# Two-layer hybrid decoder trunk: another order of the first loads, warm-up on a constant, constants in two transfers

## The chip, the cores and the metric

The kernel runs on one core of one Trainium2 chip. The metric is the device time of one execution in microseconds (us); a version's time is the median of its runs. Beside the times stands one profiled execution, whose records are quoted as rows. Engines: PE is TensorE (PEld its weight loads), ACT is ScalarE, DVE is VectorE, POOL is GpSimd, SP is SyncE; a "q" behind the name means the engine's instruction queue, which also issues transfers.

## The reference

`x` is 256 tokens by 1024 channels, float32, and there are two layers. Each layer does this, cut to what matters:

```python
hn = rms_norm(x, norm_gain)
proj = jnp.einsum('bsd,de->bse', hn, w_in)          # 1024 -> 3584 columns
a_q, a_k, a_v, a_g, b_x, b_g, c_q, c_k, c_v, c_g = jnp.split(proj, _in_split_points(), axis=-1)
y_a = dilated_attention(rope(a_q), rope(a_k), a_v) * silu(a_g)      # 8 heads of 64
y_b = rg_lru_branch(b_x, conv_w, ..., lru_lambda) * silu(b_g)       # 256 channels
y_c = stick_breaking_attention(c_q, c_k, c_v) * silu(c_g)           # 4 heads of 64
return x + jnp.einsum('bse,ed->bsd', concatenate([y_a, y_b, y_c], -1), w_out)
```

A last `rms_norm` follows the two layers. The value columns `a_v` (512 columns) and `c_v` (256 columns) are what the kernel projects first.

## The kernel before, in words

**Products.** Every float32 product of the projections is made of three fast-format products. An operand is split into a rounded part `hi` and a rest `lo`; ACT (or DVE) rounds, DVE subtracts, and PE adds hi*hi, lo*hi and hi*lo into one PSUM bank. So each weight tile that arrives costs ACT one pass, DVE one pass and PE three matmuls.

**The head of layer 0** (lines 129 to 173) is where the change lies. The 1024 channels are taken in eight steps `k` of 128. What step `k` needs comes as one packed row block `first[k]` of 128 x 1024: columns 0 to 255 are x transposed (S = 256), columns 256 to 767 the 512 value columns of `a_v`, and columns 768 to 1023 the 256 columns of `c_v`. It lands in a staging tile `st`, of which there are five in turn. Step 0 differs: its x comes with the eight columns of gains as a transfer of its own, `x0` (132 KB, line 133), and its weights as three pieces of 128 KB into `st0` (lines 134 to 136), issued in turn from ACT's and SP's queues. Steps 1 to 7 are single 512 KB transfers from SP's queue (line 147); a later one waits until the staging tile that it overwrites is free.

In a step, ACT writes `xh`, the rounded x times gain (line 155); `whi` is rounded by DVE for the 512 value columns in steps 0 and 1, in two pieces in step 0 (line 157), and by ACT for the rest (lines 159 and 161); DVE makes `xl` (line 162) and `wlo` (line 164). Step 0 is 18 matmuls of 256 columns, a later step 6 of 512 and 6 of 256 (line 171). In steps 0 and 1 PE goes through all columns for xh*hi, then for xl*hi, then for xh*lo; from step 2 on it finishes the 512 value columns first.

Before the first data is there, PE runs seven matmuls of 512 bf16 columns on a tile `cold` that DVE has set to zero (lines 129, 130 and 142). Their result is never read.

**After the head**, SP issues in this order: `prm_t`, the two halves of the first weight chunk CQ (line 107), the four pieces of `xres` (line 181), the constants `con` as one transfer of 128 x 640 (line 186), the rope table `rp` (line 399), the gate weights `gw_t` (line 401), and then the weight chunks CK and on, each in halves of 512 KB, as staging tiles come free (line 107). `con` holds a band `diag` and the identity `ident` in columns 0 to 255 and the mask `nmask` in columns 256 to 639. `ident` is first read when DVE spreads the inverse norms on a diagonal (line 380), `nmask` by the attention scores (line 525).

**Order.** PE's instructions run in the order in which the source writes them; those of the other engines are ordered by the framework's scheduler. The framework adds the waits, for data, for free buffers, and for the semaphores of its transfers.

Of the kernel before, what the change touches and what calls it, by code (L numbers as in the profile page):

```python
# [11 lines left out]
BF16 = mybir.dt.bfloat16  # L12
# [3 lines left out]
P = 128  # L16
S = 256
# [20 lines left out]
C_NM = 256  # L38
C_W = 640
# [10 lines left out]
def trunk_kernel(ctx: ExitStack, tc: tile.TileContext, x, first_x, first, wpack, prm_d, gatew, gains, consts, rope, out):  # L50
    nc = tc.nc
    act, dve, pe, gps = nc.scalar, nc.vector, nc.tensor, nc.gpsimd
# [4 lines left out]
    sb = ctx.enter_context(tc.tile_pool(name="sb", bufs=1))  # L57
# [19 lines left out]
    def table(name, behind=()):  # L77
        load = act.preload_act_table_set(name)  # L78
        for u in (*loaded["users"], *behind):
            dep(load, u)  # L80
        loaded["load"], loaded["users"] = load, []
# [44 lines left out]
        ask(l, c, ahead)  # L126
        return ready.pop((l, c))

    cold = sb.tile([P, 512], BF16, name="cold", tag="th")
    dve.memset(cold, 0.0)  # L130
    x0 = sb.tile([P, S + NK], F32, name="x0", tag="it")
    st0 = wst.tile([P, 1024], F32, name="st", tag="st")
    nc.sync.dma_start(out=x0, in_=first_x)
    act.dma_start(out=st0[:, S:S + 256], in_=first[0][:, S:S + 256])
    nc.sync.dma_start(out=st0[:, S + 256:S + 512], in_=first[0][:, S + 256:S + 512])
    act.dma_start(out=st0[:, S + 512:1024], in_=first[0][:, S + 512:1024])
    table(LN_EXP)
    av_ps = [bank(at, "s") for _ in range(NT)]
    cv_bk = [bank(pp, "pp") for _ in range(NT)]
# [42 lines left out]
    con = cst.tile([P, C_W], F32, name="con")  # L182
    ident = con[:, C_ID:C_ID + P]
    nmask = con[:, C_NM:C_NM + 384]
    diag = con[:, C_DG:C_DG + 255]
    nc.sync.dma_start(out=con, in_=consts)

    tiny_t = cst.tile([P, 48], F32, name="tiny")
    tiny = tiny_t[:, 0:1]
# [111 lines left out]
    for l in range(L):  # L301
# [254 lines left out]
        th = sb.tile([P, 2, S], F32, name="th", tag="th")  # L556
# [264 lines left out]
```

## Time and profile before

| what | value |
|---|---|
| median of 3 runs | 246.11 us (245.97 to 247.12) |
| profiled execution | 246.3 us, its recorded span 244.4 us |
| PE busy | 237.7 us, 97% of the span |
| DVE / ACT busy | 193.6 us (79%) / 170.7 us (70%) |
| first matmul on data | 4.73 us after the span's start |
| moved by transfers | 43.90 MB, mean 180 GB/s |

The profiled execution has 1.9 us outside its recorded span. Times in rows count from the span's start. A row of the timeline gives start, duration, engine, line, operation, destination and sources, and in square brackets how long the engine was idle before and what ended that. Rows that follow each other directly on one engine are merged, with their count.

### The profile page before, as it was taken

How to read it: one execution, taken by the hardware profiler on the slowest of the kernel's cores; microseconds unless marked ns; L12 is line 12 of the kernel's file. 1: busy time of each engine (PE TensorE's matmuls, PEld its weight loads, DVE VectorE, ACT ScalarE, POOL GpSimd, SP SyncE). 2: the span in 40 equal slices, each digit the busy share in tenths (PEclk: the TensorE clock that was granted, in tenths of full speed). 3: DMA queues.
4: the chain of work that ended last, by engine and by line, in shares of the span. 5: the costliest groups of instructions: out<-in, count | busy, mean ns of one | idle time of the engine just before them, and what ended most of it. 6: DMA issues, size and time to landing. Idle time of an engine off the chain costs nothing.

```text
span 244.4 us, 4800 instructions
## 1 busy us (share of the span) xinstructions
PE 237.7 (97%) x1777; PEld 213.0 (87%) x1777; DVE 193.6 (79%) x457; ACT 170.7 (70%) x371; POOL 10.9 (4%) x43
## 2 busy tenths in 40 slices
PE   7999999999999999999999999999999999999991
PEld 3889999999998899878889988888889889987881
DVE  3884699999999889986693665999999967885262
ACT  3759969628788499974672775876679749993143
POOL 0037000002000000000000000000010000000000
PEclk9999999999999999999999999999999999999999
DMA  7989989366836841277359387605471862000022
GB/s 209 400 259 388 398 279 331 119 206 182 265 119 207 310 112 71 90 237 257 107 161 258 108 305 255 200 6 192 155 215 27 241 253 86 3 0 0 3 75 97
DMA packets 14038, 43.90 MB, mean 180 GB/s; under 512 B 1728, under 2 KB 3008, under 8 KB 14016
## 3 DMA queue, kind: packets, MB, share of 16 engines
q1 hardware_dynamic: 13248, 42.43, 52.1%
q10 hardware_dynamic: 576, 0.66, 0.7%
q0 software_dynamic: 192, 0.52, 0.7%
q8 instruction: 14, 0.23, 0.4%
q14 instruction: 8, 0.07, 0.1%
HBM read 42.03 MB, written 1.05 MB: 176 GB/s over the span
## 4 chain that ended last, share of the span: by engine, by line
PE 96%; DMA 1%; ACT 1%; issue 0%; DVE 0%; DVEq 0%
PE pp L215 51%; PE pp L334 11%; PE s L215 9%; PE pp L331 5%; PE s L171 5%; PE s L465 3%; PE pp L171 2%; PE y L429 2%; PE s L518 2%; DMA x<-first_x 1%; PE s L445 1%; PE y L215 1%; PE pp L429 1%; PE s L577 1%; PE s L263 1%
## 5 line engine op out<-in xcount | busy, mean ns | idle before, releaser
L112 DVE TENSOR_TENSOR wlo<-st,whi 128x512 fp32r<-128x512 f32 x132 | 84.1, 686 | 13.9 <-ACT whi L110 13.6
L110 ACT ACTIVATE whi<-st 128x512 fp32r<-128x512 f32 x132 | 73.5, 627 | 17.1 <-PE pp L215 7.1
L215 PE MATMUL pp<-xx,whi 128*128 128x256 f32 x480 | 63.3, 285 | 0.0
L215 PEld LDWEIGHTS pp<-xx,whi 128*128 128x128 f32 x480 | 59.6, 191 | 0.8 <-issue 0.3
L215 PE MATMUL pp<-xx,wlo 128*128 128x256 f32 x240 | 33.7, 283 | 0.0
L215 PEld LDWEIGHTS pp<-xx,wlo 128*128 128x128 f32 x240 | 31.0, 192 | 0.0
L334 PE MATMUL pp<-xx,whi 128*128 128x512 f32 x112 | 29.3, 396 | 0.0
L334 PEld LDWEIGHTS pp<-xx,whi 128*128 128x128 f32 x112 | 20.1, 189 | 3.8 <-ACT scr L84 0.3
L84 ACT ACTIVATE pr<-scr,mn 128x128 f32<-128x128 f32 (+1 forms) x32 | 14.1, 442 | 6.6 <-DVE mn L525 6.6
L78 ACT ACT_TABLE_LOAD x13 | 16.7, 1283 | 1.9 <-PEq L814 1.7
L331 PEld LDWEIGHTS pp<-xx,wlo 128*128 128x128 f32 x112 | 15.3, 190 | 1.1
L331 PE MATMUL pp<-xx,wlo 128*128 128x256 f32 x112 | 15.6, 282 | 0.0
L215 PE MATMUL pp<-whi,yh 128*128 128x512 f32 (+1 forms) x48 | 13.3, 382 | 0.0
L215 PE MATMUL pp<-wlo,yh 128*128 128x512 f32 (+1 forms) x48 | 12.8, 372 | 0.0
L215 PE MATMUL pp<-whi,yl 128*128 128x512 f32 (+1 forms) x48 | 12.8, 372 | 0.0
L417 ACT ACTIVATE yh<-scr 128x512 fp32r<-128x512 f32 x8 | 5.0, 631 | 7.2 <-DVE scr L415 7.1
L215 PEld LDWEIGHTS pp<-wlo,yh 128*128 128x128 f32 x48 | 8.6, 188 | 1.6
L215 PEld LDWEIGHTS pp<-whi,yl 128*128 128x128 f32 x48 | 8.6, 188 | 1.6
L171 PE MATMUL s<-whi,xx 128*128 128x512 f32 (+1 forms) x36 | 9.6, 381 | 0.4 <-ACT xx L155 0.4
L215 PEld LDWEIGHTS pp<-whi,yh 128*128 128x128 f32 x48 | 8.3, 189 | 1.6 <-issue 0.3
L525 DVE CUSTOM_DVE_ANT_0 scr<-s,con 128x128 f32<-128x128 f32 (+1 forms) x32 | 9.2, 353 | 0.0
L337 ACT ACTIVATE low<-pp 128x256 f32<-128x256 f32 x14 | 5.3, 377 | 5.1 <-PE pp L334 5.1
(181 smaller groups left out, 364.0 us busy)
## 6 DMA issues: line engine op xcount, KB each, us to landing
st<-w_pack SPq DMA_DIRECT2D x66, 512.0 KB, 5.1
st<-first SPq DMA_DIRECT2D x7, 512.0 KB, 5.5
xres<-x_in SPq DMA_DIRECT2D x4, 256.0 KB, 7.1
gw_t<-gate_w SPq DMA_DIRECT2D x2, 256.0 KB, 5.7
gn<-gains SPq DMA_DIRECT2D x2, 256.0 KB, 5.1
xs<-xc POOLq DMA_DIRECT2D x4, 128.0 KB, 4.8
gf<-gains SPq DMA_DIRECT2D x2, 256.0 KB, 6.6
out<-st ACTq DMA_DIRECT2D x2, 192.0 KB, 2.0
```

What stands on the lines that cost most here:

```text
L78: load = act.preload_act_table_set(name)
L84: i = dep(act.activation(*a, **k), loaded["load"])
L110: split[l, c] = act.activation(hi[:, ws], st[:, ss], AF.Copy)
L112: dve.tensor_sub(lo[:, ws], st[:, ss], hi[:, ws].bitcast(F32))
L171: pe.matmul(ps[t][:, c0 - base:c1 - base], a[:, k, t * P:(t + 1) * P], b[:, c0:c1], start=k == 0 and i == 0 and c0 == base, stop=k == NK - ...
L215: pe.matmul(ps, a(k), b(k), start=first and i == 0, stop=last and i == len(seq) - 1, skip_group_check=skip)
L331: pe.matmul(ps[:, 0:S], lo[:, k, cs], xh[:, k, :], start=False, stop=False, skip_group_check=True)
L334: pe.matmul(ps, hi[:, k, cs], xx[:, k].rearrange("p h t -> p (h t)"), start=i == 0, stop=i == len(seq) - 1, skip_group_check=True)
L337: act.activation(low, ps[:, S:2 * S], AF.Copy, scale=sc)
L429: pe.matmul(y[hr, p * 128 + o:p * 128 + 256], vt[:, s0, hs], wts[i][s0], start=s0 == 0, stop=s0 == 1)
L465: pe.transpose(tp[:, i * P:(i + 1) * P], tiles[h0 + h][:, j * P:(j + 1) * P], ident)
L525: dve.tensor_tensor_reduce(xs[:, cs], sps[h][:, cs], nmask[:, cs], -0.125, 3e38, ALU.add, ALU.min, mn[:, t:t + 1])
```

## The change

All of the first transfers go on SP's queue: x0, then the 512 value columns as one piece of 256 KB, then the 256 columns. ACT issues none of them. The warm-up matmuls read a constant 1.0 that the program's preamble has put into memory, with a step of zero along the columns, so the tile `cold` and DVE's memset are gone. `con` is loaded as columns 0 to 255 and columns 256 to 639. Everything else, the two-piece rounding of line 157 and the order of PE's matmuls included, stays.

```diff
-    cold = sb.tile([P, 512], BF16, name="cold", tag="th")
-    dve.memset(cold, 0.0)
+    cold = nc.const_aps.tensor(1.0, [P, 512], BF16)
     x0 = sb.tile([P, S + NK], F32, name="x0", tag="it")
     st0 = wst.tile([P, 1024], F32, name="st", tag="st")
     nc.sync.dma_start(out=x0, in_=first_x)
-    act.dma_start(out=st0[:, S:S + 256], in_=first[0][:, S:S + 256])
-    nc.sync.dma_start(out=st0[:, S + 256:S + 512], in_=first[0][:, S + 256:S + 512])
-    act.dma_start(out=st0[:, S + 512:1024], in_=first[0][:, S + 512:1024])
+    for c in (slice(S, S + 512), slice(S + 512, 1024)):
+        nc.sync.dma_start(out=st0[:, c], in_=first[0][:, c])
...
-    nc.sync.dma_start(out=con, in_=consts)
+    for c in (slice(0, C_NM), slice(C_NM, C_W)):
+        nc.sync.dma_start(out=con[:, c], in_=consts[:, c])
```

## The prediction

> **What bounds the kernel now.** I read the page first, then the chain of waits, then the timeline of the first 14 us, where the change acts.
>
> ```profile
> span 244.4 us, 4800 instructions
> PE 237.7 (97%) x1777; PEld 213.0 (87%) x1777; DVE 193.6 (79%) x457; ACT 170.7 (70%) x371; POOL 10.9 (4%) x43
> PE 96%; DMA 1%; ACT 1%; issue 0%; DVE 0%; DVEq 0%
> ```
>
> PE is busy 97% of the span and is 96% of the chain that ends last. So only two things can move the end: when PE starts on data, and whether it stops later. From the chain, pieces with start, duration and what:
>
> ```profile
> 0.74 3.36 DMA x<-first_x
> ...
> 4.73 0.86 PE s L171 x4
> 5.97 0.47 PE s L171 x4
> ...
> 7.39 0.47 PE s L171 x2
> ...
> 9.55 1.65 PE s L171 x6
> ...
> 22.52 8.64 PE pp L215 x72
> ```
>
> The chain begins with the landing of x0 at 4.10 and is PE's from 4.73 on. Step 0 ends at 7.39, step 1 at 9.55, and the head at 22.52, where CQ's products follow. The timeline shows what else stands close to that chain:
>
> ```profile
> 0.31 0.10 POOL L814 MEMSET const-bfloat16-1.0<- 128x1 bf16 x1
> 0.74 0.41 ACTq L134 DMA_DIRECT2D st<-first  x1
> 0.74 0.37 SPq L133 DMA_DIRECT2D x<-first_x  x1
> 0.86 0.27 DVE L130 MEMSET cold<- 128x256 uint32 x1 [0.86 <-PEq L814]
> 1.17 0.42 SPq L135 DMA_DIRECT2D st<-first  x1
> 1.18 0.45 ACTq L136 DMA_DIRECT2D st<-first  x1
> 1.19 3.17 PE L142 MATMUL y<-cold 128*128 128x512 bf16 x7 [1.19 <-DVE cold L130]
> 1.64 9.14 SPq L147 DMA_DIRECT2D st<-first  x7
> 4.29 0.29 DVE L157 CAST whi<-st 128x256 fp32r<-128x256 f32 x1 [3.00 <-DMA st<-first]
> 4.75 0.29 DVE L157 CAST whi<-st 128x256 fp32r<-128x256 f32 x1 [0.16 <-DMA st<-first]
> 4.96 0.48 DVE L162 SCALAR_TENSOR_TENSOR xx<-x,xx 128x256 fp32r<-128x256 f32 x1
> 5.00 0.42 ACT L159 ACTIVATE whi<-st 128x256 fp32r<-128x256 f32 x1 [0.37 <-DMA st<-first]
> 5.81 0.63 PE L171 MATMUL s<-whi,xx 128*128 128x256 f32 x4
> 6.24 0.51 ACT L155 ACTIVATE xx<-st,x 128x256 fp32r<-128x256 f32 x1 [0.82 <-DMA st<-first]
> 8.18 0.51 ACT L155 ACTIVATE xx<-st,x 128x256 fp32r<-128x256 f32 x1 [1.12 <-DMA st<-first]
> 8.59 0.83 ACT L161 ACTIVATE whi<-st 128x768 fp32r<-128x768 f32 x1
> 9.48 1.19 PE L171 MATMUL s<-whi,xx 128*128 128x512 f32 x4
> ```
>
> ACT and DVE wait for transfers in steps 0, 1 and 2 (the brackets at 4.29, 5.00, 6.24 and 8.18). Step 2 lands at 8.18, and ACT has its whi ready at 8.59 + 0.83 = 9.42; PE starts on it at 9.48, just where step 1 leaves off. So two nearly equal chains meet at 9.5: PE's own progress through steps 0 and 1, and the landing of step 2 with ACT's two passes. After that ACT needs 1.34 us a step (0.51 + 0.83) and PE 2.16 (7.39 to 9.55), and PE stays the bound. **Whatever the change gains before 9.4 is lost again at 9.4 unless step 2 lands earlier too**; a loss on either chain goes to the end.
>
> **The change part by part.** *First transfers.* The bytes are the same. What limits them is the stream, in us, then per window (PE, PEld, DVE, ACT, POOL busy), clock, DMA share and GB/s last:
>
> ```profile
> 0.00:2.00 2.00, 0.81 (x2) 0.28 (x3) 0.43 (x4) 0.34 (x1) 0.43 (x9) 1.00 0.18 17
> 2.00:3.00 1.00, 1.00 (x4) 0.43 (x3) 0.00 (x0) 0.94 (x1) 0.00 (x0) 1.00 0.88 127
> 3.00:4.00 1.00, 1.00 (x4) 0.18 (x2) 0.00 (x0) 0.00 (x0) 0.00 (x0) 1.00 1.02 338
> 4.00:5.00 1.00, 0.63 (x3) 0.30 (x2) 0.55 (x3) 0.51 (x2) 0.00 (x0) 1.00 1.05 411
> 5.00:5.50 0.50, 0.50 (x5) 0.33 (x3) 0.50 (x3) 0.42 (x1) 0.00 (x0) 1.00 1.00 320
> 5.50:6.00 0.50, 0.50 (x5) 0.50 (x5) 0.50 (x2) 0.00 (x0) 0.00 (x0) 1.00 1.05 336
> 6.00:7.00 1.00, 1.00 (x11) 1.00 (x10) 0.97 (x4) 0.76 (x2) 0.00 (x0) 1.00 0.90 365
> ```
>
> The share is about 1 from 2 us on, so the DMA engines have work all the time, and a second queue adds none of it. Summed, 34 kB have moved by 2 us, 161 by 3, 499 by 4, 910 by 5, 1070 by 5.5, 1238 by 6 and 1603 by 7. Step 0 is 528 kB (x0 135, three pieces of 131), moved by 4.07; its last piece is used at 5.00, 0.93 later. Step 1 (1052 kB) is moved by 5.45 and used at 6.24, 0.8 later. Step 2 (1577 kB) is moved by 6.93 and used at 8.18, 1.25 later. With one queue the order becomes x0, 512 columns, 256 columns. An estimate by the same sums with a lag of 0.85: x0 moved by 2.8, landed about 3.65 (0.45 earlier); the 512 columns (397 kB) moved by 3.70, landed about 4.55; the 256 columns, steps 1 and 2 have the same bytes ahead as before, so 5.0, 6.24 and 8.18.
>
> DVE's first rounding then starts at 4.57 instead of 4.29 and ends 4.86, the second ends 5.15 instead of 5.04, xl 5.63 instead of 5.44, and wlo moves by 0.2 too. PE's first matmul moves from 4.73 to about 4.95, but the third part of step 0 still waits for ACT's whi (5.00 + 0.42 = 5.42, as before), and xl at 5.63 is in time for 5.81. So step 0 ends where it ended: **0.0 us**. Both ends: if the single piece lands only at 5.00, with the rest of step 0 (its latest, by the row at 5.00), the roundings end 5.6, xl 6.08, and xl's matmuls start 0.32 late, of which the 0.1 us before 9.48 take a part: +0.25. If step 2's lag shrinks from 1.25 to the 0.8 of step 1, whi is ready at 8.97; then PE's progress decides, and that saves at most the stalls of step 0. At 0.47 for four matmuls of 256 columns, 18 take 2.1 us where step 0 took 2.66 (4.73 to 7.39): −0.55. I take 0, which is what unchanged bytes ahead of step 2 give.
>
> *Issuing.* SP issues one piece more ahead of step 1. Its issues come 0.47 apart (1.17 to 1.64), so step 1 is issued at about 2.11 and step 4 at 3.5. Step 1's bytes are reached at 4.07, and x0's were moving within 1.3 us of their issue (34 kB by 2.0), so 2.11 + 1.3 = 3.4 is early enough: 0. If the cover were gone, the price would be that 0.47 on step 2's landing, so on the end. ACT loses two issues (0.41 and 0.45); it has nothing to round before x0 lands, so 0.
>
> *Warm-up.* DVE's memset (0.27) goes, and with it PE's wait until 1.19. The constant is written at 0.31 by POOL, and SP and ACT pass the preamble at 0.74, so PE starts at about 0.78 and the 3.17 us end at 3.95 instead of 4.36. Nothing waits for them: 0, except for the clock (below).
>
> *Constants in two transfers.* One issue more on SP. The rows of SP's queue and of its waits (line, what it waited for, us in total, times, longest):
>
> ```profile
> 17.22 0.65 SPq L399 DMA_DIRECT2D rp<-rope  x1
> 18.63 0.33 SPq L401 DMA_DIRECT2D gw_t<-gate_w  x1
> 19.89 0.33 SPq L107 DMA_DIRECT2D st<-w_pack  x1
> SPq L401 <- DMA st<-w_pack: 0.7, 1, 0.7
> xres<-x_in SPq DMA_DIRECT2D x1, 256.0 KB, 7.1
> 26.06 5.84 ACT L110 ACTIVATE whi<-st 128x512 fp32r<-128x512 f32 x10
> L616 DVE TENSOR_TENSOR rp<-rp,rb x2: 416/417/418, 35.6 to 35.9; 128x256 f32<-128x256 f32 x2
> ```
>
> gw_t reads nothing from w_pack, yet its issue waits 0.7 us for a w_pack transfer: CQ's first half, the eighth transfer before it. So I read that a transfer waits for the one eight places earlier. With one transfer fewer ahead and one more in con, the eighth before rp is now CQ's first half: rp is issued at 18.63 instead of 17.22, gw_t behind CQ's second half, and CK's first half behind the first xres piece, which was issued at 13.35 and takes 7.1: about 20.5 instead of 19.89. rp is first read at 35.6: 0. CK is rounded by ACT from 26.06, without a wait in that row, and the stream ahead of it is as long as before; at worst it comes 0.6 late, and PE takes CK's first columns only when CQ's 48 matmuls from 22.52 are done (0.12 each by the chain's 72 in 8.64), at 28.3. So 0, and at most +0.3 if DVE's rests come late as well. The first half of con lands earlier, but the waits name no one who waits for con, so no gain.
>
> The sum is 0 on the profiled 246.3, which is 0.2 above the median; against the median that is **246.1 us**.
>
> **The rivals.** *A, the head gets shorter.* Step 2's lag shrinks, or less interleaving lets the whole head go earlier: at most the 0.55 above, about 245.6. For it: 1.25 against 0.8 shows that some lag is avoidable. Against it: the share is already 1.
>
> *B, slower: the clock.* PE's warm-up covers 1.19 to 4.36 and leaves 0.37 to the first matmul; now it covers 0.78 to 3.95 and leaves about 1.0. Four matmuls of 256 columns take 0.86 us at 4.73 and 0.47 at 5.97, so up to about 5 us PE ran at about half pace (part of the 0.86 is waiting for data), and the warm-up was just long enough. If with the longer hole the full pace came only at time t, all work from 4.95 on would run at half pace and lose (t − 4.95)/2; none of it is absorbed, since PE is the bound. It decides (over 1.2 us) from t = 7.4; at t = 8.2 it gives 1.6 us, 247.7. Against it: PE is idle in neither case for more than 1 us. The profile's clock reads 1.00 in every window of the head, so it can't settle the matter.
>
> The Trainium skill (TensorE: Matmul & The Clock Gate, Part 1) says the clock goes up after one busy window of about 3.4 us, and that these windows run freely, so that the moment varies from run to run. By that rule a hole inside the window counts against it, and a kernel with the hole would sometimes lose up to one window at half clock, 1.7 us; by the rows alone the sum stays 0. The trace agrees as far as it shows anything: the warm-up lasts 3.17 us, and the full pace is there by 5.97. The 1.15 us between the runs of before is as large as such a slip would be, but no run here shows its cause.
>
> *C, the order of ACT and DVE changes.* Only PE's order is fixed; with other first transfers the scheduler may put one pass ahead of a needed one. The price is one pass of 0.6 to 0.8 us each time, either way: 245.4 or 246.8; past 0.5% only if it happens twice.
>
> *D, the change doesn't do what it says:* PE still waits for something until 1.19. Then the clock is as before, and 246.1 stays.
>
> **How the numbers follow.** Forecast (with D) 0.63, A 0.15, B 0.12, C 0.10. About 0.5% (1.2 us) is what a measurement of this kernel can tell from no change. The forecast and A lie inside it wholly; B is beyond it in three of four cases (0.09), C in half of them, evenly by sign. With a little for what I overlook: faster 0.05, same 0.83, slower 0.12. The range goes from A's 245.6 less 0.3 for the spread of a median, 245.3, to the lower part of B, 247.2.
>
> **What would show each step.** In the profile after: x0's landing near 3.65; the first DVE rounding at 4.5 to 4.6, in direct sequence with the second; PE's first matmul near 4.95 and the first step-2 matmul at 9.48 as before; the warm-up from 0.78; rp issued after CQ's landing near 18.6, CK near 20.5; no new idle time on PE behind 9.5. Wrong would make it: step 2 on ACT at another time than 8.18, four 256-column matmuls taking 0.86 us still after 6 us, or another order of passes on ACT.

## The result, and the profile after

The changed kernel is slower. On the chip of the first comparison it took 248.28 us (median of 8 runs, 247.57 to 249.56) against 246.20 for the kernel before (245.97 to 247.28); the ratio is 1.0074, 95% interval 1.0053 to 1.0095. On another chip it was 247.83 against 246.46, 1.0054 (1.0034 to 1.0074). The profiled execution took 247.57 us with a span of 245.7. From its page and its chain of waits:

```profile
span 245.7 us, 4798 instructions
PE 238.8 (97%) x1777; PEld 214.6 (87%) x1777; DVE 193.6 (79%) x456; ACT 171.2 (70%) x371; POOL 11.0 (4%) x43
...
0.74 2.76 DMA x<-first_x
...
4.07 0.48 DVE xx L160
4.55 0.21 DVE whi L155
...
4.90 1.20 PE s L169 x4
6.10 0.43 PE pp L169 x2
6.52 0.85 PE s L169 x4
...
9.08 0.50 PE s L169 x2
...
11.21 1.37 PE s L169 x6
...
23.80 6.24 PE pp L214 x52
```

PE is still 97% busy, so the loss isn't idle time. CQ's products begin at 23.80 instead of 22.52, and the span is longer by the same 1.3 us: in this execution everything was lost in the head. Four matmuls of 256 columns took 0.47 us in step 0 at 5.97 before; here they take 0.85 at 6.52. Step 0 takes 4.18 us (4.90 to 9.08) instead of 2.66. PE runs at half pace through the whole of step 0. The windows of this profile read a clock of 1.00 there too, but they say nothing about this stretch: the first record of the granted clock in the trace is its rise to full, and it stands at 9.03 us here, at 4.28 before. From the timeline:

```profile
0.78 3.15 PE L140 MATMUL y<-const-bfloat16-1.0 128*128 128x512 bf16 x7 [0.78 <-PEq L813]
2.10 9.21 SPq L145 DMA_DIRECT2D st<-first  x7
3.52 0.51 ACT L153 ACTIVATE xx<-x 128x256 fp32r<-128x256 f32 x1 [1.51 <-DMA x<-first_x]
4.47 0.49 DVE L155 CAST whi<-st 128x256 fp32r<-128x256 f32 x2
4.90 1.20 PE L169 MATMUL s<-whi,xx 128*128 128x256 f32 x4 [0.98 <-DVE whi L155]
7.48 0.51 ACT L153 ACTIVATE xx<-st,x 128x256 fp32r<-128x256 f32 x1 [1.85 <-DMA st<-first]
8.72 0.51 ACT L153 ACTIVATE xx<-st,x 128x256 fp32r<-128x256 f32 x1 [0.42 <-DMA st<-first]
11.05 1.08 PE L169 MATMUL s<-whi,xx 128*128 128x512 f32 x4
```

The warm-up ends at 3.93, and PE then pauses 0.98 us. Step 1 is first used at 7.48 instead of 6.24, step 2 at 8.72 instead of 8.18, and PE starts on step 2 at 11.05 instead of 9.48. The stream is thin while step 1 should be coming (windows as before, GB/s last):

```profile
3.00:4.00 1.00, 0.92 (x3) 0.01 (x1) 0.00 (x0) 0.48 (x1) 0.00 (x0) 1.00 0.82 192
4.00:5.00 1.00, 0.10 (x1) 0.13 (x1) 0.90 (x4) 0.03 (x1) 0.00 (x0) 1.00 0.90 291
```

Before it was 338 and 411 GB/s there. Behind the head, SP's queue and ACT's passes on CK:

```profile
18.82 0.33 SPq L398 DMA_DIRECT2D rp<-rope  x1
20.06 0.33 SPq L400 DMA_DIRECT2D gw_t<-gate_w  x1
20.77 18.88 SPq L107 DMA_DIRECT2D st<-w_pack  x12
SPq L398 <- DMA st<-w_pack: 1.0, 1, 1.0
26.98 1.15 ACT L110 ACTIVATE whi<-st 128x512 fp32r<-128x512 f32 x2 [0.35 <-DMA st<-w_pack]
28.66 1.15 ACT L110 ACTIVATE whi<-st 128x512 fp32r<-128x512 f32 x2 [0.53 <-DMA st<-w_pack]
```

rp now waits for a w_pack transfer, and so CK is issued 0.9 us later. ACT, which went through ten passes from 26.06 without a wait, now waits for CK's first half and again for its second. Here PE is so late that this costs nothing more; in other executions it does, as the experiments show.

### The profile page after: what moved, and what is told of

The parts are those of the page before. It is cut to its first block, busy times and chain, and to the rows that moved or that the text cites. A ratio compares the mean times of both kernels' runs of the same rounds, so it can differ in the third digit from the quotient of the medians.

```text
span 245.7 us, 4798 instructions
## 1 busy us (share of the span) xinstructions
PE 238.8 (97%) x1777; PEld 214.6 (87%) x1777; DVE 193.6 (79%) x456; ACT 171.2 (70%) x371; POOL 11.0 (4%) x43
## 4 chain that ended last, share of the span: by engine, by line
PE 96%; DMA 1%; ACT 1%; DVE 0%; issue 0%; DVEq 0%
PE pp L214 50%; PE pp L333 11%; PE s L214 9%; PE pp L330 5%; PE s L169 5%; PE s L464 3%; PE pp L169 3%; PE y L428 2%; PE s L517 2%; PE s L444 1%; PE y L214 1%; DMA x<-first_x 1%; PE pp L428 1%; PE s L576 1%; PE s L262 1%
## 5 line engine op out<-in xcount | busy, mean ns | idle before, releaser
L169 PE MATMUL s<-whi,xx 128*128 128x512 f32 (+1 forms) x36 | 10.1, 405 | 1.0 <-DVE whi L155 1.0
L169 PEld LDWEIGHTS s<-whi,xx 128*128 128x128 f32 x36 | 6.8, 226 | 2.4 <-ACT xx L153 1.9
```

The source lines that it names most:

```text
L169: pe.matmul(ps[t][:, c0 - base:c1 - base], a[:, k, t * P:(t + 1) * P], b[:, c0:c1], start=k == 0 and i == 0 and c0 == base, stop=k == NK - ...
```

## The experiments

Single runs scatter by 2 to 3 us, the kernel before included (245.5 to 248.6 over all comparisons), so what counts is the ratio to the kernel before on the same chip, with its interval, and the rows of the one profiled execution.

| kernel | ratio (95% interval) | step 1 / step 2 first used |
|---|---|---|
| e1: changed, warm-up as before | 1.0032 (1.0008 to 1.0057) | 7.12 / 8.41 |
| e2: changed, nine warm-up matmuls | 1.0028 (1.0003 to 1.0053) | 7.57 / 8.81 |
| e3: before, constant warm-up | 0.9994 (0.9969 to 1.0018) | 5.70 / 8.33 |
| e4: before, first transfers on SP | 1.0020 (0.9996 to 1.0044) | 6.91 / 8.18 |
| r1: changed again | 1.0054 (1.0034 to 1.0074) | 6.79 / 8.52 |
| r2: before, constants in two | 1.0044 (1.0023 to 1.0065) | 6.40 / 7.85 |
| r3: changed, 768 columns in one piece | 1.0031 (1.0006 to 1.0056) | 6.02 / 7.77 |
| r4: changed, x0 from ACT | 1.0039 (1.0021 to 1.0057) | 5.97 / 8.34 |
| s1: changed, one piece, mask late | 1.0037 (1.0015 to 1.0058) | 6.21 / 7.73 |
| s2: changed, mask late | 1.0039 (1.0017 to 1.0061) | 7.01 / 8.44 |
| s3: e3 with four warm-up matmuls | 1.0032 (1.0012 to 1.0053) | 5.66 / 7.79 |
| s4: e3 with nine | 0.9998 (0.9976 to 1.0020) | 6.06 / 8.09 |
| t1: s1 with nine | 0.9995 (0.9975 to 1.0016) | 6.23 / 8.37 |
| t2: s2 with nine | 1.0024 (0.9998 to 1.0050) | 7.02 / 8.27 |
| t3: s4 with constants in two | 1.0038 (1.0008 to 1.0069) | 6.13 / 8.18 |
| t4: r2 with gw_t late | 1.0019 (0.9995 to 1.0042) | 6.04 / 7.92 |

**One part at a time.** The first four undo or make one part of the change each. e1 puts the zeroed tile back:

```diff
-    cold = nc.const_aps.tensor(1.0, [P, 512], BF16)
+    cold = sb.tile([P, 512], BF16, name="cold", tag="th")
+    dve.memset(cold, 0.0)
```

> The changed kernel with the warm-up as it was: DVE's memset of zeros is back, so the seven matmuls run from about 1.19 to 4.36 again, and the transfers stay as changed. Theory H (the clock: the pause between the warm-up's end and the first product on data grew from 0.37 to 0.98 us, and PE runs at half pace far into step 1): the pause is about 0.54 (4.36 to 4.90), most of the loss goes, median 246.4 to 247.0, step 0 takes about 2.7 instead of 4.2 us. Theory Q (one queue: steps 1 and 2 land 1.24 and 0.54 us later): median stays 248.0 to 248.5. Theory V (the constant itself, its ones or its step of zero, doesn't count as work for the clock): as H.

e2 is the changed kernel with `WARM = 9`.

> The changed kernel with nine warm-up matmuls on the constant instead of seven: they run from 0.78 to about 4.8, up to the first product on data. H: the pause is gone, median 246.3 to 246.9, with step 0 at full pace; what is left over the kernel before is the later landing of step 2 (0.55 us at most). Q: 248.0 to 248.5, no change. V: 248, no change, step 0 at half pace as in the changed kernel.

e3 is the kernel before with the constant in place of the tile, and e4 the kernel before with the changed kernel's two pieces on SP.

> The kernel before with the warm-up on the constant alone; transfers as before. The warm-up runs from 0.78 to 3.93, first data product at 4.73 or a little later: a pause of 0.8. H: 247.3 to 248.3. Q: 246.2, no change. V: 248, the whole loss.

> The kernel before with the first transfers alone changed: all on SP's queue, the 512 columns as one piece; warm-up on zeros from 1.19, constants as one transfer. H: the pause is about 0.5, median 246.2 to 246.8. Q: 247.5 to 248.3, with step 1 used near 7.5 and step 2 near 8.7 us instead of 6.24 and 8.18.

None came out as a single theory wanted it. e1 and e2 stand between H and Q, so a part of the loss is left without the longer pause. e3 cost nothing, against H's forecast: in its profile the data came earlier, so that its pause was 0.35 us and not 0.8. V isn't settled here; t3 below settles it. e4 has step 1 late as Q wanted, but a ratio that can't be told from 1.

**The constants, and why step 1 is late.** r1 is the changed kernel itself.

> The changed kernel itself, to stand beside the next three on one chip. If the later landing of step 1 is the whole loss: a ratio to the kernel before near 1.003, as with the two kernels that shared only the single queue (1.0032 and 1.0020). If the longer pause before the first product on data costs on top of it: 1.006 to 1.009, with single runs up to 3 us over the fastest.

r2 is the kernel before with the change's two transfers for `con`, and nothing else.

> The kernel before with the constants alone in two transfers. Every theory: no change, ratio 0.998 to 1.002, PE without new idle time behind the head; were the shifted waits of SP's queue a cost, 1.002 to 1.004.

This I had wrong: 1.0044. ACT's passes on CK and PE's matmuls in r2:

```profile
27.14 2.45 ACT L110 ACTIVATE whi<-st 128x512 fp32r<-128x512 f32 x4 [1.36 <-DMA st<-w_pack]
...
28.34 0.30 PEld L216 LDWEIGHTS pp<-xx,whi 128*128 128x128 f32 x2 [0.22 <-ACT whi L110]
29.12 0.30 PEld L216 LDWEIGHTS pp<-xx,whi 128*128 128x128 f32 x2 [0.48 <-ACT whi L110]
29.64 1.26 PEld L216 LDWEIGHTS pp<-xx,whi 128*128 128x128 f32 x10 [0.22 <-ACT whi L110]
...
19.41 0.33 SPq L402 DMA_DIRECT2D gw_t<-gate_w  x1
20.45 9.00 SPq L107 DMA_DIRECT2D st<-w_pack  x6
```

ACT waits 1.36 us for CK, and PE's weight loads wait for ACT three times, 0.92 us in these rows. The head of r2 was 0.25 us ahead of the kernel before at CQ, its last matmul 0.91 behind: 1.16 us lost, all between 28 and 31.

r3 and r4 bring step 1's issue back to 1.64, one with a single queue and one with two:

```diff
-    for c in (slice(S, S + 512), slice(S + 512, 1024)):
-        nc.sync.dma_start(out=st0[:, c], in_=first[0][:, c])
+    nc.sync.dma_start(out=st0[:, S:1024], in_=first[0][:, S:1024])
...
-    nc.sync.dma_start(out=x0, in_=first_x)
+    act.dma_start(out=x0, in_=first_x)
```

(the first edit is r3, the second r4).

> The changed kernel with all 768 weight columns of step 0 as one piece behind x0, still all on SP's queue, so that step 1 is issued at 1.64 again instead of 2.10. Theory Qa (the later issue makes step 1 late): step 1 is used near 6.4, the time drops by 0.5 to 1.0 us against the changed kernel. Theory Qb (one queue alone leaves the DMA engines without work after step 0): step 1 is used at 7.0 to 7.5 all the same, and between 3.5 and 5 us the stream falls below 250 GB/s; the time stays within 0.3 us of the changed kernel's.

> The changed kernel with x0 alone issued from ACT's queue: two queues at the start, step 1 issued from SP at 1.64. Qa: step 1 near 6.4. Qb: step 1 near 6.2, with 330 GB/s or more between 3 and 5 us, and x0 landing later than 3.5 since the 512 columns share the engines. Both: ratio to the kernel before 1.001 to 1.004, with the pause left.

Qb falls. In r3, with SP's queue alone:

```profile
1.64 1.96 SPq L144 DMA_DIRECT2D st<-first  x4
6.02 0.51 ACT L152 ACTIVATE xx<-st,x 128x256 fp32r<-128x256 f32 x1 [1.31 <-DMA st<-first]
3.00:4.00 1.00, 0.92 (x3) 0.01 (x1) 0.48 (x1) 0.35 (x1) 0.00 (x0) 1.00 1.04 346
4.00:5.00 1.00, 0.27 (x2) 0.30 (x3) 0.71 (x3) 0.42 (x1) 0.00 (x0) 1.00 0.98 360
```

One queue feeds the engines well enough when step 1 is issued at 1.64. By the table, the seven profiles with the extra issue (the changed kernel's, e1, e2, e4, r1, s2, t2) use step 1 at 6.79 to 7.57, 7.13 on average; the eleven others at 5.66 to 6.40, 6.06 on average. The two groups don't overlap: 0.46 us later in issue is 1.07 us later in use, and 0.43 at step 2 (8.48 against 8.05). But r3 and r4 gained little time (1.0031 and 1.0039), since they kept the constants' extra transfer and the pause. In their profiled executions the pause (0.81 and 0.88 us) cost nothing: CQ's products began at 22.11 and 22.57, as early as before or nearly so, and what was lost was lost at CK.

**Taking both away.** s2 moves the mask half of `con`, first read at 62.5 us, behind CK's products; s1 has that and r3's single piece.

```diff
-    for c in (slice(0, C_NM), slice(C_NM, C_W)):
-        nc.sync.dma_start(out=con[:, c], in_=consts[:, c])
+    nc.sync.dma_start(out=con[:, 0:C_NM], in_=consts[:, 0:C_NM])
...
             scaled(kc, ck_ps)
+            nc.sync.dma_start(out=con[:, C_NM:C_W], in_=consts[:, C_NM:C_W])
```

> The changed kernel with both suspected costs taken away and SP's single queue and the warm-up on the constant kept: the 768 weight columns of step 0 as one piece, so that step 1 is issued at 1.64, and the mask half of the constants issued only behind CK's products. Theory M (two costs in the head: the extra issue ahead of step 1, and the constants' extra transfer, which by the wait for the transfer eight places earlier makes CK late): ratio 0.997 to 1.002, CK's third pass on ACT at 27.2 or earlier, no PE gap at 28 to 31 us. Theory H (the longer pause before the first product): 1.004 or more, since the pause is as in the changed kernel.

> The changed kernel with the mask half of the constants issued only behind CK's products, nothing else. M: CK's third pass on ACT near 27 instead of 28.7; the ratio falls from 1.0054 to 1.001 to 1.003, which is what the later step 1 costs alone. H: 1.004 or more. If the constants' extra transfer costs nothing in this kernel, since PE is late at CK anyway: 1.0054 stays.

s2 missed M's forecast: 1.0039, with CK's third pass at 28.13 and not near 27. s1 went as H wanted, not M. Its step 1 and its CK are on time, and still it stands at 1.0037, with its profiled execution at half pace (the chain of waits):

```profile
4.75 1.20 PE s L168 x4
5.94 0.43 PE pp L168 x2
6.37 0.85 PE s L168 x4
...
7.65 0.85 PE s L168 x4
8.50 0.43 PE pp L168 x2
8.93 0.85 PE s L168 x2
```

s3 and s4 change the warm-up's length alone, on e3 (`WARM = 4` and `WARM = 9`).

> The kernel before with the warm-up on the constant, and four matmuls instead of seven: it ends near 2.65, so the pause before the first product is about 2. H: PE starts on data at half pace nearly always, up to one window of 3.4 us; 0.3 to 1.2 us slower than the same kernel with seven (ratio 1.002 to 1.005). M: no change against seven, ratio 0.998 to 1.001.

> The kernel before with the warm-up on the constant, and nine matmuls: it runs from 0.78 to 4.8, up to the first product. H: 0.2 to 0.5 us faster than with seven and than before, ratio 0.998 to 0.999. M: no change, ratio 0.999 to 1.001, or a little slower where the first product would have started before 4.8.

s3's first product comes 1.59 us after its warm-up and runs at half pace (0.85 for four at 5.85); 1.0032 against 0.9998 with nine, as H said, though nine isn't measurably better than e3's seven.

**Three costs?** The last four tell the costs apart. t1 and t2 are s1 and s2 with `WARM = 9`, t3 is s4 with the constants in two transfers, and t4 is r2 with `gw_t` of layer 0 issued behind CK's products.

> The kernel with both head costs undone (768 columns of step 0 as one piece, mask issued late, SP's queue alone, constant warm-up) and nine warm-up matmuls instead of seven: no pause before the first product. H (the pause is the third cost): the ratio falls from 1.0037 to 0.997 to 1.001. If the pause is no cost and something else is left: 1.003 to 1.004 stays.

> The changed kernel with the mask half issued late and nine warm-up matmuls: only the extra issue ahead of step 1 is left. If the late step 1 costs by itself: 1.001 to 1.003, with step 1 used at 6.8 to 7.5. If it was only the pause that cost: 0.998 to 1.000.

> The kernel before with the constants in two transfers, the constant warm-up and nine matmuls: no pause, step 1 early, only the constants' extra transfer left. If it costs by itself: 1.002 to 1.005, with PE gaps at 28 to 31 us and CK's third pass on ACT at 28 or later. If not: 0.998 to 1.001.

> The kernel before with the constants in two transfers, and gw_t of layer 0 issued behind CK's products instead of ahead of CK's load, so that CK's first half again waits for the same transfer as in the kernel before (and has 256 KB less ahead of it). If the constants' cost is CK's later load: the ratio falls from 1.0044 to 0.998 to 1.001 and the PE gaps at 28 to 31 us go. If it is the extra transfer as such, anywhere: 1.003 or more stays.

t1 is the clearest. Two more warm-up matmuls take it from 1.0037 to 0.9995, and its twelve runs lie within 246.14 to 246.83, where s1's went from 246.32 to 248.40. The timeline of t1:

```profile
0.78 4.00 PE L139 MATMUL y<-const-bfloat16-1.0 128*128 128x512 bf16 x9 [0.78 <-PEq L812]
4.71 0.82 PE L168 MATMUL s<-whi,xx 128*128 128x256 f32 x4
5.60 0.64 PE L168 MATMUL s<-whi,xx 128*128 128x256 f32 x4
7.04 0.63 PE L168 MATMUL s<-whi,xx 128*128 128x512 f32 x2
```

No pause, and step 0 is done at 7.04. In t3 the clock rose at 3.49, before the first product on data:

```profile
0.78 3.43 PE L141 MATMUL y<-const-bfloat16-1.0 128*128 128x512 bf16 x9 [0.78 <-PEq L814]
```

Nine warm-up matmuls took 3.43 us there and 4.00 in t1, so full pace came on the constant's matmuls alone, and V falls as well. t3 also shows the constants' cost with no pause before the first product (1.0038). t2 leaves the late step 1 alone: 1.0024, which like e4's 1.0020 isn't beyond its interval. t4 goes in the expected direction, and CK is issued at 19.62 instead of r2's 20.45, but ACT still waits 1.21 us for CK's second half at 28.15:

```profile
19.62 8.48 SPq L107 DMA_DIRECT2D st<-w_pack  x6
25.79 1.15 ACT L110 ACTIVATE whi<-st 128x512 fp32r<-128x512 f32 x2
28.15 1.15 ACT L110 ACTIVATE whi<-st 128x512 fp32r<-128x512 f32 x2 [1.21 <-DMA st<-w_pack]
```

So the shifted wait is shown to delay CK's issue, not to be all of the constants' cost. Nor is that last wait the extra transfer's alone: s2, whose second transfer comes behind CK, waits 1.08 us for CK's second half too. t1 is level with the kernel before, and no version here beats it measurably.

**Where each execution lost its time.** Set beside the kernel before matmul by matmul, every profile keeps from 33 us to its last matmul the offset that it has there, within 0.03 us. So all is lost in the head or at CK. At CK, six of the nine profiles with the constants' second transfer ahead of it lost 0.9 us or more (r2 and t3 1.2); the eight others lost 0.3 at most. In the head the changed kernel's profile, s1, s2 and s3 lost 0.7 to 1.5 us; of the others the best gained 0.4, and the worst (e2) lost 0.9.

**When the clock rises.** The same four are the profiles in which the clock rose last, at 8.46 to 9.65 us (elsewhere at 3.49 to 6.96). Each trace records the clock's rise to full and its fall at the end. In all 18 traces the two lie either 238.93 or 235.52 us apart; the difference, 3.41 us, goes into them 70 and 69 times. So the clock changes only at the ends of windows of 3.41 us, and where these lie differs from execution to execution. In all 18 the rise ends the first window in which PE was busy for 2.71 us or more, and no window with 2.70 or less brought it. One such window each from the changed kernel, s2, t3 and r3 (start and end, length, PE's busy time), and r3's first products:

```profile
2.20:5.61 3.41, 2.43 (x8) 1.03 (x6) 1.51 (x4) 0.91 (x2) 0.00 (x0) 1.00 0.93 286
2.26:5.68 3.42, 2.70 (x9) 1.36 (x8) 1.93 (x5) 0.92 (x2) 0.00 (x0) 1.00 0.97 270
0.08:3.49 3.41, 2.71 (x7) 1.02 (x8) 0.24 (x3) 1.28 (x1) 0.43 (x9) 1.00 0.51 118
0.82:4.24 3.42, 3.10 (x7) 0.80 (x7) 0.71 (x4) 1.71 (x2) 0.14 (x5) 1.00 0.65 208
...
4.73 0.71 PE L168 MATMUL s<-whi,xx 128*128 128x256 f32 x4 [0.81 <-ACT whi L156]
```

The first two windows hold the whole pause, and the clock rose one window later, at 9.03 and 9.09. The last two ended with the rise. So a pause costs only where it falls into the window that would otherwise have brought the rise; in r3 it fell mostly behind that window, in r4 (rise at 3.59) wholly. r1, the changed kernel once more, had its data early: a pause of 0.38 us, the rise at 4.37, and 246.64 us for that execution. And without a pause the rise can be late: in e1 it came at 6.74, since PE had begun at 1.19 and the window that ended at 3.33 held only 2.13 us of its work.

## Why the prediction was wrong

Three terms stood at 0 in the sum. Two of them cost time beyond their intervals, the constants' second transfer and the clock, which the step on the warm-up left to rival B; the third, the later issue of step 1, made step 1 late, but its cost by itself isn't clear of noise.

**What it had right.** The landing of x0 (3.65 forecast, used at 3.52), the first rounding (4.57; 4.47), the first product (4.95; 4.90), the warm-up (0.78 to 3.95; 0.78 to 3.93) and the waits in SP's queue (rp 18.63, CK about 20.5; 18.82 and 20.77) came as forecast. That PE is the bound throughout, and that the change gains nothing, held too. The agreement at x0 is partly luck: in the nine other profiles with x0 first on SP's queue and nothing on ACT's it was used at 2.84 to 3.21, and in r1, the same kernel, the first product came at 4.30.

**Step "Issuing", costed at 0.** It took step 1's bytes to be in time at 3.4 although issued 0.46 us later. They weren't: the stream fell to 192 GB/s, and step 1 came 1.07 us later on average. The price named there for a lost cover, 0.47 at step 2, was right (0.43). The saturated share of the windows before was read as a property of the chip, where it was a property of that order of issues. What it costs by itself is 1.0020 to 1.0024, not beyond the intervals.

**Step "Constants in two transfers", costed at 0 with +0.3 at most.** The mechanism, a wait for the transfer eight places earlier, was right; the size wasn't. The step held that CK's landing would not follow its issue, because the stream ahead was as long as before. In r2 CK's first pass on ACT is at 27.14 instead of 26.06, and PE loses 1.16 us; r2 and t3 measure 1.0044 and 1.0038, about 1 us. By the rows of before the cover was about 1.6 us for CK's first quarter (rounded by 26.7, needed at 28.3) and, by an estimate, 0.6 for its last (four passes of 0.58 end at 28.4; needed six matmuls after the first, at 29.0). A delay of 1.1 us used that up.

**The clock, given a chance of 0.12 as rival B.** In the profiled execution step 0 took 4.18 us instead of 2.66 at half pace; at full pace PE would have had to wait there too, for step 1 until about 8, so clock and late step 1 share that loss. B's own formula gives 2.0 us for a rise at 9.03, and the head lost 1.3. That the pause brings the late rise is shown by s1 against t1, by s3 against s4 and by the windows above. B's argument against itself, that PE is never idle for more than 1 us, is what failed: 0.7 to 1.0 us of pause is enough where it falls into the wrong window, and how often it does isn't measured. The Trainium skill (TensorE: Matmul & The Clock Gate, Part 1) has the rule behind it: free-running windows of about 3.4 us that must be busy. The traces agree: their windows are 3.41 us long, and the one that brought the rise was always busy for 2.71 us or more. It fits that e3, whose pause was short in its profile (0.35 us, rise at 3.94), lost nothing.

The costs don't add up. Apart they are about 0.2, 0.4 and 0.4%, and together 0.5 to 0.7%, since PE, late from one, no longer waits for the other: the changed kernel's profile has the head's loss and none at CK, e1's and r2's have it at CK. Rival A (a shorter head) didn't show. Rival C (another order of passes) did, in small: DVE's xl pass moved ahead of the two roundings, as x0 landed first, and the chain of waits runs through it. The 512 columns, issued at 1.17, took 3.1 us to land, so the roundings could have begun at about 4.27 instead of 4.47: at most 0.2 us of the first product.

## What to carry to other kernels

A transfer costs its queue an issue and a place in the row of transfers that later ones wait for, and that can bind far from where it was added: count the issues ahead of the first transfer that PE waits for, and those between a late weight and the transfer it queues behind. A warm-up should reach to the first product; starting it earlier is worth nothing if it ends so early that the pause behind it costs the clock a window. Where several such covers are thin, a profile shows only the one that binds in that execution, so take them away together before judging one.

## What the runs showed of the hardware that was not expected

The windows' clock reads 1.00 while four 256-column matmuls take 0.85 us instead of 0.47, because the trace has no record of the clock before its rise: until then pace has to be read from the matmuls. That rise came at 3.49 to 9.65 us in the 18 profiles, always at the end of the first window of 3.41 us in which PE was busy for about 2.7 us or more. A transfer of 512 KB issued 0.46 us later was used 1.07 us later at the start of the kernel; why it is more than the issue's own delay stays open, and so does what else delays CK's second half in t4. With the pause gone the scatter of the runs shrank from 2.1 us (s1) to 0.7 (t1); that the moment of full pace is the source of most scatter isn't shown, for s4, also without a pause, scatters by 2.0.
